# Layer 1: the first of two projections woven into the attention is no longer pinned to score products

## The chip, the cores and the metric

The kernel runs on one core of one Trainium2 chip. The metric is the device time of one execution in microseconds (us). A time given for a kernel is the median of its runs. The profile is of one execution more, and a program's order of instructions on every engine is fixed when it is built: each engine takes its own list from the front.

## The reference

A two-layer backbone over 1024 latent tokens (a grid of 16 rows and 64 columns) and 256 context tokens, model width 1024, all in fp32. Each layer normalizes its input, scales and shifts it, projects it to queries, keys, values and gates, mixes, projects back, and adds to the stream. Layer 0 (even) has two attentions, one global and one in a band. Layer 1 (odd), where the change is, has a convolution branch and a neighbourhood attention, in parallel:

```
def odd_mixer(...):
    cv, cgl, cg, dq, dk, dv, dg = split_cols(h_lat @ w_in, ODD_WIDTHS)
    x_cv, x_cgl, x_cg, x_dq, x_dk, x_dv, x_dg = split_cols(h_ctx @ w_in, ODD_WIDTHS)
    oc = conformer_conv(cv, cgl, cg, dw_w, dw_b, ln_g, ln_b)
    ...
    def d_row(args):      # one grid row of 64 queries, 8 rows of keys around it, 16 columns wide
        bias = rpb[:, dr_idx][:, :, dc_idx] + col_mask[None, None]
        kk = jnp.concatenate([c_dk, kr], axis=1)
        vv = jnp.concatenate([c_dv, vr], axis=1)
        return gqa_attend(qr[:, :, :, None, :], kk, vv, bias)
    ...
    y_lat = jnp.concatenate([oc, od * jax.nn.silu(dg)], axis=-1) @ w_out
```

The attention has 8 heads of width 64. Each query sees the 256 context keys and a window of 8 x 16 grid keys with a bias from a table.

## The kernel before, in words

**Arithmetic.** Every fp32 matrix product is made of three matmuls. An operand is split into a high part (a cast on ScalarE, line 308) and a low part (a subtraction on GpSimd or VectorE, line 311), and `mm3` (lines 328 to 330) issues high x high, high x low and low x high. A weight block is loaded by `load_w` (line 338): a DMA into `wr` (two buffers), a cast to `wh`, a subtraction to `wl` (four buffers each, which hold one block of four pairs of rows).

**The projections of layer 1.** `d_proj(i)` (line 1126) projects heads 2i and 2i+1. With a first weight block it makes Q for the two halves of the latent tokens, then K for both halves and for the context (the matmuls that read `hc`). With a second block it makes, for each half, V and the gate, then V of the context, each followed by small transposes. Each of these ten products takes 24 matmuls: 512 columns wide, 256 for the context. Results leave through the PSUM tag `pp` (two banks), are split on ScalarE and VectorE (`spq`, `spk`, `spv`) and stored to DRAM (`QD`, `KD`, `VD`, `GD`) by the sync queue. `d_proj` is a generator: it yields three times in each product, after two, five and eight of its eight steps of three matmuls, and once more near its end, 31 yields in all. `d_proj(0)` runs beside the convolution and `d_proj(1)` beside the layer norm that follows it. `d_proj(2)` and `d_proj(3)` are woven into the attention.

**The attention of layer 1.** 16 groups (8 heads, two halves of the grid's columns) of seven key tiles each. A group is prepared by `attn_prep` (line 399): three tables `bm` are loaded (two buffers, line 1271), and in `maxes` (line 1296) products `mx` of keys and queries (lines 1304 and 1312) are reduced to row maxima on VectorE (lines 1306 and 1313, the latter with a table `bm` as input). `attn_fin` (line 426) transposes the maxima (`trn`, line 433) and writes them into the query tile `QL` (line 434). Only then can a key tile's score product be finished: it consists of two matmuls into a PSUM bank `st` (two banks), one with `QH` (line 505) and one with `QL` (line 509). A bias is added on VectorE (line 514), ScalarE takes the exponential (line 515, or 517 for the context tiles), the result is split into `ph` and `pl`, and up to three tiles later `flush` issues the three matmuls `ov` with V (lines 456 to 458).

**What sets the order.** The code traces all instructions in one sequence, each with a priority (its place in that sequence). A scheduler then draws up each engine's list, by dependences, buffers and a timeline of its own: of what it holds to be ready, the lowest priority number goes first. Three things steer it. `later(FL[1])`, with FL[1] = -98, gives the woven projection the priority that it would have 98 instructions earlier. `weave` (line 538) advances the attention `nmain` times and spreads `nfill` steps of the projection over these advances. The attention's first 14 advances are the preparation of two groups; from then on every second advance traces one key tile's score product. And a lag pins the projection's matmuls:

```
def weave(main, nmain, fill, nfill, last=True, all_fill=True, lag=0):
    ...
        while done * nmain < (k + 1) * nfill:
            with ExitStack() as cx:
                cx.enter_context(later(FL[layer[0]]))
                if lag and len(sts) >= lag:
                    cx.enter_context(tc.issue_after(sts[-lag].ins))
                next(fill, None)
            done += 1
```

`sts` is the list of all score products traced so far (their first matmuls, line 505), layer 0's too. `issue_after` puts what the step issues on that product's engine, TensorE, behind that product in TensorE's list. It is an order, not a wait for a result, and it does not touch the step's casts, subtractions and DMAs. With a lag of 6, a step cannot be issued ahead of the sixth last score product traced. The calls are

```
weave(main, WV[0], d_proj(2), 31, False, True, LAG[0])     # WV[0] = 77
weave(main, WV[1], d_proj(3), 31, False, True, LAG[1])     # WV[1] = 45
```

and after these the output projection is woven in with LAG[2] and LAG[3].

Of the kernel before, what the change touches and what calls it, by code (L numbers as in the profile page):

```python
# [51 lines left out]
OHQ = 0  # L52
PCB = 3
FL = (80, -98)
LAG = (6, 6, 6, 12)
FIN = (2, 2)
WV = (77, 45, 85, 24, 12)
SQ = (0, 1)
# [30 lines left out]
def tile_kernel(ctx: ExitStack, tc: tile.TileContext, a, out):  # L89
# [448 lines left out]
    def weave(main, nmain, fill, nfill, last=True, all_fill=True, lag=0):  # L538

        done = 0  # L540
        for k in range(nmain):
            next(main, None)
# [7 lines that stand above are left out]
        if all_fill:  # L550
            for _ in fill:
                pass
        if last:
            for _ in main:
                pass
# [458 lines left out]
    with ExitStack() as l1x:  # L1014
# [331 lines left out]
        def out1_alloc():  # L1346
            for c in range(2):
                ocs.append(bigp.tile([P, 2, 4, 512], F32R, tag="big", name=nm("oc")))
            for c in range(2):
                x2.append(bigp.tile([P, DK, 512], F32, tag="big", name=nm("x2")))  # L1350
                od3.append(pair("od3"))
            for c in range(2):
                for f in range(4):
                    lo = ocs[c][:, 1, f, :]
                    SC.dma_start(lo.bitcast(F32), Oc[:, f, c * 512 : (c + 1) * 512])

        def out1_split():
            for _ in range(2):
                yield
            for f in range(4):  # L1360
                for c in range(2):
                    lo = ocs[c][:, 1, f, :]
                    with behind():
                        split(lo.bitcast(F32), ocs[c][:, 0, f, :], lo, "s", "gv"[c])
                if f % 2:
                    yield
# [8 lines left out]
        def od_load(hf):  # L1375
            od[hf] = bigp.tile([P, 2, 3, 512], F32R, tag="big", name=nm("od"))
            for f in range(3):
                split(yo[:, f, hf], od[hf][:, 0, f, :], od[hf][:, 1, f, :], "s", ODE)
# [24 lines left out]
        def out1_part(fs, ks=(0, 1)):  # L1403
            for e2 in range(4):
                w = load_w(wp, a["od_wo"], e2, 256, WB, dks=fs)
                for e in (2 * e2, 2 * e2 + 1):
                    if fs[0] == 0:
                        x2_load(e)
                    for k in ks:
                        yield from out1(fs, e, k, *w)  # L1410
# [59 lines left out]
        main = attn_gen(dlow, groups1, VSH, LOOK1, {11: [], 12: [13, 14], 13: [15]})  # L1470
        weave(main, WV[0], d_proj(2), 31, False, True, LAG[0])
        weave(main, WV[1], d_proj(3), 31, False, True, LAG[1])
        out1_alloc()
        weave(main, WV[2], chain(out1_split(), out1_part(range(4))), 36, False, True, LAG[2])
        assert fin[0] >= 12
        for hf in (1, 0):
            od_load(hf)
        weave(main, WV[3], out1_part((4, 5, 6), (1,)), 8, False, True, LAG[3])
        assert fin[0] >= 14
# [127 lines left out]
```

## Time and profile before

| | |
|---|---|
| three runs | 1565.89, 1562.34, 1564.85 us |
| median | 1564.85 us |
| profiled execution, its time | 1560.63 us |
| its span, first to last instruction | 1558.8 us |
| granted TensorE clock, mean | 0.967 of full speed |

TensorE's busy time counts a matmul from its start to a modelled end, and matmuls overlap: two of 512 columns start about 0.23 us apart and each is shown as 0.39 us long. So a stretch in which TensorE is shown busy throughout can still go at half speed; the granted clock beside it tells that. A row of the order of time gives the start, the length, the engine, the line, and in brackets the idle time before it with what ended it. A name such as `hc`, `hh` or `hl` is an input of the projections (context, high and low part of the latent tokens); `p` is a projection's PSUM tile.

### The profile page before, as it was taken

What the parts mean: (1) busy time and instruction counts of PE and PEld (TensorE: products, weight loads), DVE (VectorE), ACT (ScalarE), POOL (GpSimd) and SP (SyncE); (2) the same over time, 40 slices, a digit from 0 to 9 for tenths busy, and PEclk for the clock granted to TensorE, in tenths of its full rate; (3) what the DMA queues carried; (4) which work ended last, traced back from release to release, by engine and by line L of the source; (5) the groups of instructions that cost most, each with busy time, mean ns of one, the idle gap of its engine ahead of it and who ended that gap; (6) DMA issues with size and microseconds to landing.
All of it is one profiled execution on the core that took longest, in us unless ns stands there. A gap on an engine that the chain in (4) does not pass through costs nothing.

```text
span 1558.8 us, 21469 instructions
## 1 busy us (share of the span) xinstructions
PE 1458.2 (94%) x7084; PEld 1172.0 (75%) x7084; DVE 1053.0 (68%) x2113; ACT 746.6 (48%) x1418; POOL 799.6 (51%) x637
## 2 busy tenths in 40 slices
PE   6899999998998989999999878999999799989995
PEld 2786977896896768876866656888887688868875
DVE  2833557589579865466677946999756566577866
ACT  3721434444435565447556663443434355555563
POOL 3430434455445765557556664665632334364675
PEclk9899999999999999999999989999999899989996
DMA  9474315422312245122112012111446777878632
GB/s 363 160 240 132 106 58 182 143 70 91 118 51 78 94 159 169 54 68 54 47 31 92 7 50 81 51 52 41 149 159 204 208 220 227 256 218 241 182 111 108
DMA packets 154169, 199.83 MB, mean 128 GB/s; under 512 B 14717, under 2 KB 95817, under 8 KB 154057
## 3 DMA queue, kind: packets, MB, share of 16 engines
q1 hardware_dynamic: 147392, 186.88, 38.3%
q10 hardware_dynamic: 6664, 11.57, 2.2%
q8 instruction: 56, 0.92, 0.3%
q14 instruction: 57, 0.46, 0.1%
HBM read 148.07 MB, written 49.02 MB: 126 GB/s over the span
## 4 chain that ended last, share of the span: by engine, by line
PE 74%; DVE 14%; issue 4%; DMA 3%; POOL 2%; ACT 2%; SPq 0%; DVEq 0%; POOLq 0%; ACTq 0%
PE p L328 7%; PE p L329 7%; PE p L330 7%; PE ov L456 4%; PE ov L458 4%; PE ov L457 4%; PE po L329 4%; PE po L328 4%; PE po L330 4%; PE st L505 4%; PE st L509 4%; PE pq L328 2%; PE pq L329 2%; PE pq L330 2%; PE pg L328 2%
## 5 line engine op out<-in xcount | busy, mean ns | idle before, releaser
L311 POOL TENSOR_TENSOR pl<-pf,ph 128x512 fp32r<-128x512 f32 (+4 forms) x321 | 395.2, 1242 | 375.6 <-ACT ph L308 326.3
L517 ACT ACTIVATE pf<-st 128x512 f32<-128x512 f32 x284 | 166.3, 597 | 211.3 <-PE st L509 169.4
L311 POOL TENSOR_TENSOR wl<-wr,wh 128x512 fp32r<-128x512 f32 (+2 forms) x131 | 170.6, 1314 | 144.7 <-ACT wh L308 125.8
L308 ACT CAST ph<-pf 128x512 fp32r<-128x512 f32 (+4 forms) x364 | 209.1, 588 | 27.1 <-PE ov L457 16.9
L328 PE MATMUL p<-hh,wh 128*128 128x512 f32 x448 | 177.6, 397 | 5.6 <-ACT hh L308 2.8
L329 PE MATMUL p<-hl,wh 128*128 128x512 f32 x448 | 176.0, 394 | 1.2 <-POOL hl L311 1.2
L330 PE MATMUL p<-hh,wl 128*128 128x512 f32 x448 | 173.4, 393 | 0.0
L505 PE MATMUL st<-QH,KAt 128*128 128x512 f32 (+4 forms) x364 | 141.5, 390 | 8.9 <-ACT pf L517 8.1
L456 PE MATMUL ov<-ph,Vt 128*128 128x512 f32 (+4 forms) x364 | 141.1, 388 | 5.2 <-DVE y L666 3.9
L458 PE MATMUL ov<-pl,Vt 128*128 128x512 f32 (+4 forms) x364 | 141.1, 388 | 1.8 <-POOL pl L311 1.4
L457 PE MATMUL ov<-ph,Vt 128*64 128x512 f32 (+4 forms) x364 | 139.0, 382 | 0.0
L509 PE MATMUL st<-QL,KBt 68*128 68x512 f32 (+4 forms) x364 | 136.5, 386 | 1.9 <-DVE QL L434 1.8
L1079 DVE SCALAR_TENSOR_TENSOR cps<-U,taps,cps 128x512 f32<-128x512 f32 x184 | 126.4, 751 | 0.9
L308 ACT CAST wh<-wr 128x512 fp32r<-128x512 f32 (+2 forms) x134 | 81.1, 613 | 94.5 <-DMA wr<-in_od_d_dram 18.0
L328 PEld LDWEIGHTS p<-hh,wh 128*128 128x128 f32 x448 | 84.8, 189 | 24.2 <-ACT hh L308 3.0
L329 PEld LDWEIGHTS p<-hl,wh 128*128 128x128 f32 x448 | 84.9, 190 | 19.3 <-POOL hl L311 2.2
L330 PEld LDWEIGHTS p<-hh,wl 128*128 128x128 f32 x448 | 85.0, 190 | 17.3
L629 DVE TENSOR_REDUCE mp<-mx 128x1 f32<-128x512 f32 x128 | 85.3, 681 | 16.6 <-PE mx L628 15.7
L328 PE MATMUL pq<-wh,hh 128*128 128x384 f32 x256 | 88.5, 346 | 2.8 <-ACT hh L308 2.8
L505 PEld LDWEIGHTS st<-QH,KAt 128*128 128x128 f32 x364 | 69.7, 192 | 26.5 <-ACT pf L517 11.6
L948 DVE SCALAR_TENSOR_TENSOR x<-po,modT,x 128x512 f32<-128x512 f32 (+1 forms) x72 | 47.0, 657 | 62.2 <-PE po L330 61.3
L329 PE MATMUL pq<-wl,hh 128*128 128x384 f32 x256 | 87.6, 342 | 0.0
(280 smaller groups left out, 3473.1 us busy)
## 6 DMA issues: line engine op xcount, KB each, us to landing
mw<-in_mod_w_dram SPq DMA_DIRECT2D x16, 1024.0 KB, 5.6
Q<-qs SPq DMA_DIRECT2D x40, 256.0 KB, 2.2
QH<-Q SPq DMA_DIRECT2D x80, 128.0 KB, 2.8
mw<-in_mod_w_dram SPq DMA_DIRECT2D x16, 512.0 KB, 6.8
wr<-in_od_d_dram SPq DMA_DIRECT2D x32, 256.0 KB, 3.6
wr<-in_ev_qkv_dram SPq DMA_DIRECT2D x16, 384.0 KB, 5.3
KAt<-KD SPq DMA_DIRECT2D x16, 384.0 KB, 5.6
wr<-in_od_wo_dram SPq DMA_DIRECT2D x22, 256.0 KB, 3.4
```

What stands on the lines that cost most here:

```text
L308: acts.append(SC.copy(hi, src))
L311: (GP if leng == "g" else VE).tensor_tensor(lo, src, hi.bitcast(F32), op=ALU.subtract)
L328: PE.matmul(o, lh, rh, start=first, stop=False)
L329: PE.matmul(o, lh, rl, start=False, stop=False)
L330: PE.matmul(o, ll, rh, start=False, stop=last)
L456: PE.matmul(o, V[:, 64:192], ph[:, :n], start=(t == 0), stop=False)
L457: PE.matmul(g.ov[0:64, q0 : q0 + n], V[:, 0:64], ph[:, :n], start=False, stop=False)
L458: PE.matmul(o, V[:, 64:192], pl[:, :n], start=False, stop=(last and g.sink is None))
L505: sts.append(PE.matmul(st[:, :n], KA[:, cs], g.QH[:, q0 : q0 + n], start=True, stop=False))
L509: PE.matmul(st[:, :n], KB[0:68, cs], g.QL[0:68, q0 : q0 + n], start=False, stop=True)
L517: acts.append(SC.activation(pf[:, :n], st[:, :n], AF.Exp, scale=1.0 if g.bias else SCALE))
L1079: VE.scalar_tensor_tensor(pc, uc, w, pc, op0=ALU.mult, op1=ALU.add)
```

## The change

One constant: the lag of the first weave, that of `d_proj(2)`, goes from 6 to 0. With 0, `weave` skips the `issue_after`. The priority of 98 instructions earlier stays, as do the lags of the other weaves and all instructions.

```
-LAG = (6, 6, 6, 12)
+LAG = (0, 6, 6, 12)
```

## The prediction

> **What bounds the kernel now.** I read the page first, then busy time by stretches around the place of the change, then TensorE's instructions in order of time, then the waits and the chain there.
>
> ```profile
> span 1558.8 us, 21469 instructions
> ...
> PE 1458.2 (94%) x7084; PEld 1172.0 (75%) x7084; DVE 1053.0 (68%) x2113; ACT 746.6 (48%) x1418; POOL 799.6 (51%) x637
> ...
> PE 74%; DVE 14%; issue 4%; DMA 3%; POOL 2%; ACT 2%; SPq 0%; DVEq 0%; POOLq 0%; ACTq 0%
> ```
>
> TensorE is the bound: 74% of the chain that ended last. An order of work can win only where TensorE stands still or runs at a lower clock. The stretches in which the first woven projection runs (columns: stretch, length, busy of PE, PEld, DVE, ACT, POOL, then granted clock, DMA share, GB/s):
>
> ```profile
> 1212.00:1216.00 4.00, 2.88 (x12) 1.80 (x10) 2.79 (x8) 0.85 (x2) 0.00 (x0) 1.00 1.09 270
> 1216.00:1220.00 4.00, 0.47 (x1) 0.19 (x1) 0.49 (x1) 0.00 (x0) 0.00 (x0) 0.66 1.09 374
> 1220.00:1224.00 4.00, 2.64 (x5) 1.37 (x5) 3.29 (x10) 0.00 (x0) 0.00 (x0) 0.50 0.51 154
> 1224.00:1228.00 4.00, 2.17 (x8) 1.57 (x8) 2.13 (x6) 0.94 (x2) 0.00 (x0) 0.50 0.42 112
> 1228.00:1232.00 4.00, 4.00 (x17) 3.58 (x17) 2.73 (x5) 2.91 (x7) 3.49 (x4) 0.63 0.27 75
> 1230.00:1281.00 51.00, 51.00 (x279) 43.78 (x279) 33.10 (x82) 31.08 (x63) 24.64 (x24) 0.99 0.70 200
> 1281.00:1362.00 81.00, 81.00 (x432) 69.12 (x431) 48.97 (x116) 40.36 (x84) 32.67 (x30) 1.00 0.82 250
> ```
>
> There is a hole from 1213 to 1228, with the clock down to half. After it TensorE is full without a break through both woven projections, up to 1362. TensorE's own order in and behind the hole:
>
> ```profile
> 1210.73 0.28 PE L505 MATMUL st<-QH,KAt 128*128 128x256 f32 x1
> 1210.85 0.40 PE L328 MATMUL p<-hh,wh 128*128 128x512 f32 x1
> 1211.09 0.40 PE L329 MATMUL p<-hl,wh 128*128 128x512 f32 x1
> ...
> 1213.15 0.39 PE L1304 MATMUL mx<-KAt,QH 128*128 128x256 f32 x2
> 1213.86 0.96 PE L1312 MATMUL mx<-KAt,QH 128*128 128x320 f32 x2 [0.31 <-DVE mp L1313]
> 1215.26 0.50 PE L1304 MATMUL mx<-KAt,QH 128*128 128x256 f32 x2 [0.44 <-DVE mp L1313]
> 1216.54 0.47 PE L1312 MATMUL mx<-KAt,QH 128*128 128x440 f32 x1 [0.78 <-DVE mp L1306]
> 1220.99 0.73 PE L1312 MATMUL mx<-KAt,QH 128*128 128x440 f32 x1 [3.98 <-DVE mp L1313]
> ...
> 1223.41 0.64 PE L1312 MATMUL mx<-KAt,QH 128*128 128x320 f32 x1 [0.27 <-DVE mp L1306]
> ...
> 1226.22 0.98 PE L509 MATMUL st<-QL,KBt 68*128 68x512 f32 x2 [1.83 <-DVE QL L434]
> ...
> 1228.13 0.49 PE L509 MATMUL st<-QL,KBt 68*128 68x352 f32 x1
> 1228.43 0.41 PE L328 MATMUL p<-hc,wh 128*128 128x256 f32 x1
> ...
> 1230.13 0.63 PE L509 MATMUL st<-QL,KBt 68*128 68x512 f32 x1
> 1230.56 0.55 PE L1312 MATMUL mx<-KAt,QH 128*128 128x440 f32 x1
> ...
> 1232.22 0.31 PE L509 MATMUL st<-QL,KBt 68*128 68x320 f32 x1
> 1232.37 0.28 PE L328 MATMUL p<-hc,wh 128*128 128x256 f32 x1
> 1232.49 0.28 PE L329 MATMUL p<-hc,wh 128*128 128x256 f32 x1
> ```
>
> The attention cannot start. Its row maxima (mx) are reduced on VectorE with tables that a DMA brings (bm, two buffers), and the second halves of the score products (L509) need those maxima in QL. Two products' first halves have taken both st banks, so no third score product can be issued before 1226. What makes the hole, from the waits (total, times, longest) and then from the chain (start, length):
>
> ```profile
> POOL pl L311 <- ACT ph L308: 27.7, 1, 27.7
> ACT pf L517 <- PE st L509: 11.8, 1, 11.8
> ...
> DVE mx L1313 <- DMA bm<-in_d_bm_dram: 4.7, 2, 3.9
> ```
>
> ```profile
> 1215.05 5.19 DMA bm<-in_d_bm_dram
> ...
> 1222.48 2.19 DMA bm<-in_d_bm_dram
> ```
>
> **Does the pin hold work back here?** By the code, the weave spreads 31 steps of the projection over 77 advances of the attention. The first 14 advances are preparation, then every second one traces a key tile. Counting both from 0, step 11 is traced when 7 tiles are, and is pinned behind tile 1; step 12 behind tile 2 (8 traced), step 13 behind tile 4 (10 traced). Steps 0 to 9 are pinned behind products of layer 0, long done. The trace agrees at each place: nine matmuls start right behind tile 1's product (1210.85); the next, the context part of K (hc), stand still over the whole hole and start at 1228.43, right behind tile 2's pair; the next nine at 1232.37, right behind tile 4's. So the pin is what leaves the hole empty. hc's weights were already there, being those of the K matmuls before it.
>
> **The sum, on the profiled execution.** Its own time is 1560.63 us (span 1558.8 and 1.8 around it); the median of the three runs shown, 1564.85, is 4.2 higher. The forecast is the difference put on that median. The measurement can tell about 0.2%, 3.1 us, from no change.
>
> *Removed:* an order on TensorE alone. No instruction goes or comes; loads, casts and stores were never pinned, but they wait for the matmuls that free their buffers and so move with them.
>
> *Room in the hole:* the idle pieces above, 0.31 + 0.44 + 0.78 + 3.98 + 0.27 + 1.83 = 7.6 us. Besides, from 1226.22 to 1230.56 the products start 0.43 us apart (1230.13 to 1230.56) where warm ones start 0.24 apart (1210.85 to 1211.09): 4.3 us of work that takes 2.4 warm, so 1.9 more. Together 9.5.
>
> *What can fill it:* K's context part, 24 matmuls 0.12 apart (1232.37 to 1232.49): 2.9 us. Then the first V block, 24 at 0.24: 5.8. Together 8.7. V needs the second weight block:
>
> ```profile
> L311 POOL TENSOR_TENSOR wl<-wr,wh 128x512 fp32r<-128x512 f32 x6 | 7.7, 1294 | 4.2 <-ACT wh L308 2.9 <-PE p L329 1.3
> ...
> L308 ACT CAST wh<-wr 128x512 fp32r<-128x512 f32 x6 | 3.7, 614 | 4.3 <-DMA wr<-in_od_d_dram 2.8 <-PE p L329 1.4
> ```
>
> ```profile
> wr<-in_od_d_dram SPq DMA_DIRECT2D x8, 256.0 KB, 4.3
> ```
>
> Its buffers come free as hc's matmuls pass, from about 1214.3. Each of four pairs then takes a cast of 0.61 and a subtraction of 1.29. ScalarE and GpSimd idle there for 11.8 and 27.7 us, so this is hidden; had they been full, it would cost 4 x 1.9. Two raw pairs are staged by their two buffers. The other two must be loaded: about 1215 + 4.3 + 1.9 = 1221.2, inside the hole. So 8.7 us of fill fits, by data. The DVE half of hc's split and its store on SP also move in; VectorE waits 3.9 us there itself.
>
> *What comes through:* work done in the hole is gone from the full stretch behind it, but the attention must be able to use that. Score products per stretch (first halves, the x in brackets), and the last idle piece of the one in which the attention ran almost alone:
>
> ```profile
> 1227.50:1281.00 53.50, 8.54 (x23) 4.65 (x24) 0.97 0.68 193
> ...
> 1353.00:1373.00 20.00, 3.71 (x10) 1.88 (x10) 0.91 0.86 263
> 1362.00:1381.00 19.00, 3.48 (x8) 1.78 (x8) 0.82 1.00 278
> ```
>
> ```profile
> 1378.50 0.77 PE L1304 MATMUL mx<-KAt,QH 128*128 128x256 f32 x2 [3.71 <-DMA KAt<-KD]
> ```
>
> Now it goes at 53.5/23 = 2.33 us a tile, TensorE full. With 8.7 us less work TensorE would allow 44.8/23 = 1.95. Almost alone, the attention managed 20/10 = 2.0, and in the other stretch 19/8 = 2.38, or 1.91 without the 3.71 us wait for K, which this stretch does not have. With fill still between, neither end is reached: I take 2.1, nearer to 2.0, because that row has the fewer foreign waits. That gives 23 x (2.33 - 2.1) = 5.2 us. Ends: 23 x (2.33 - 2.0) = 7.5, and nothing at 2.38.
>
> *What it costs:* two weight loads of 256 KB come while the DMA engines are full (1.09 and 374 GB/s at 1216 to 1220), together with the bm tables on which the chain waits: 524 KB / 374 GB/s = 1.4 us on that chain. Between none and this I take all.
>
> *Sum:* -5.2 + 1.4 = -3.8 us: 1556.8 for the profiled execution, **1561.0 us** against the median. Behind 1281 the second projection is still pinned and TensorE full (81.00 of 81), so the shift should reach the end. What is late next is the attention's own chain.
>
> **A rule of the skill that speaks against it.** The row of 3.98 us shows the head of TensorE's order waiting and nothing passing it. The Trainium skill, "TensorE: Matmul & The Clock Gate", Part 3 ("What overlaps and what doesn't"), says that matmuls keep program order strictly, only weight loads may run ahead; this case's trace agrees as far as the 3.98 us row goes. By it, a V matmul put into the hole and waiting for its weights would hold up the maxima behind it; that is rival C (1570.0 against 1561.0).
>
> **The rivals.**
> A, all of it comes through: the attention keeps up at 1.95 us a tile and the loads disturb nothing. For it: VectorE is busy 33.1 and ScalarE 31.1 of 51 us there. Against: no stretch shows a pace under 2.0 without taking a wait out. Gain 8.7 to 9.5: about 1555.7.
> B, it is given back: freed of pins, the fill is used up before tile 26, and the second projection still waits behind tile 26. The attention then runs alone, at 2.38 a tile with a lowered clock (0.82 in that row). At a mean pace of 2.33 nothing is left: 1564.85, or 1566.3 with the loads' 1.4.
> C, slower: V matmuls stand in the order ahead of the maxima, and their last weight pair comes late. The maxima wait for bm until 1220.24 (1215.05 + 5.19); the last pair is ready at about 1221.2 undisturbed, 1223.9 with a further subtraction of 1.3 and the 1.4 of contention. It decides when the pair is later than bm: up to 3.7 us on the attention's start, with nothing gained since TensorE waits too; with the loads' 1.4 added to bm's second round, 5.1: 1570.0.
> That the pin does nothing is excluded by the three places above.
>
> **How the numbers follow.** Forecast (gain 1 to 7.5) 0.48; A 0.11; B 0.21; C 0.20. Of the forecast's own range about three quarters lie beyond 3.1 us: faster 0.36 + 0.11 = 0.47. Same: the other 0.12 and most of B, 0.18: 0.30. Slower: C and a little of B: 0.23. The range runs from 1553.5, the whole room of 9.5 and 1.8 more for half the spread of the runs shown (1562.34 to 1565.89), to 1568.5, short of C's end; the forecast's own is 1557.3 to 1563.9.
>
> **What would show it.** Right: hc matmuls between 1213 and 1220, no idle piece near 4 us before the first L509, the clock near 1 in 1216 to 1228, no full stop of TensorE up to the end of the second projection, which ends 3 to 5 us earlier. Loads: bm's wait on VectorE longer than 4.7 us. B: idle TensorE just before tile 26, and the second projection starting at the same time as now. C: TensorE waiting for wl or wh in the hole, and the first L509 later than 1226.2. The forecast is wrong if the hole stays open, or if it fills and the second projection's end does not move.

## The result and the profile after

| | before | after |
|---|---|---|
| median | 1562.34 us (11 runs) | 1571.16 us (11 runs) |
| lowest to highest | 1558.21 to 1565.89 | 1565.62 to 1573.50 |
| profiled execution, its time | 1560.63 us | 1567.64 us |
| its span | 1558.8 us | 1565.9 us |

The changed kernel is slower: ratio 1.0048, 95% interval 1.0033 to 1.0064. The forecast was 3.8 us faster: 1561.0 us, put on the median of the three runs shown with it (1564.85), with a range from 1553.5 to 1568.5. A ratio here and below is worked out over all executions and is not the quotient of the two medians; three single executions far out (2052.9 us of the kernel before, 3605.55 of e1_lag12, 3608.42 of e12_wv) are left out of the ratios.

The page of the changed kernel: span, busy time, and the shares of the chain of waits that ended last. The totals hardly say more than that the span grew by 7.1 us, so the places have to be read.

```profile
span 1565.9 us, 21471 instructions
...
PE 1463.2 (93%) x7084; PEld 1174.2 (75%) x7084; DVE 1049.3 (67%) x2113; ACT 748.0 (48%) x1418; POOL 803.0 (51%) x637
...
PE 74%; DVE 14%; DMA 4%; issue 3%; POOL 2%; ACT 1%; SPq 0%; DVEq 0%; POOLq 0%; ACTq 0%
```

The changed kernel by stretches (stretch, length, busy time of PE, PEld, DVE, ACT and POOL with instruction counts, granted clock, DMA share, GB/s). The first five answer to the same stretches of before; the others were chosen from the order below.

```profile
1212.00:1216.00 4.00, 4.00 (x29) 3.72 (x29) 1.63 (x4) 1.82 (x4) 0.78 (x1) 1.00 1.11 324
1216.00:1220.00 4.00, 4.00 (x23) 3.49 (x23) 1.83 (x5) 0.55 (x2) 1.77 (x2) 1.00 1.08 371
1220.00:1224.00 4.00, 4.00 (x20) 3.31 (x19) 1.91 (x7) 0.77 (x2) 1.29 (x1) 1.00 0.81 254
1224.00:1228.00 4.00, 4.00 (x21) 3.32 (x20) 1.51 (x5) 0.47 (x1) 1.29 (x1) 1.00 0.63 162
1228.00:1232.00 4.00, 3.19 (x18) 2.35 (x17) 2.69 (x8) 2.79 (x6) 0.00 (x0) 1.00 0.38 104
1231.00:1255.00 24.00, 24.00 (x135) 20.64 (x133) 13.81 (x32) 13.83 (x28) 10.18 (x10) 1.00 0.55 171
1254.80:1289.40 34.60, 26.98 (x97) 18.82 (x95) 23.52 (x60) 16.69 (x35) 14.55 (x15) 0.75 0.77 215
1289.00:1371.00 82.00, 81.74 (x422) 69.14 (x422) 46.54 (x112) 40.23 (x82) 29.68 (x28) 0.98 0.75 222
```

The hole is closed: TensorE is full from 1212 to 1228 and the clock is 1.00, where it was down to 0.50. But a new slack stretch stands at 1254.8 to 1289.4: TensorE busy 27.0 of 34.6 us at a clock of 0.75. TensorE's order of time in the changed kernel shows how the one led to the other:

```profile
1185.66 1.05 PE L265 MATMUL bc<-ident,nr 128*128 128x128 f32 x8
...
1213.66 0.29 PE L328 MATMUL p<-hc,wh 128*128 128x256 f32 x1
...
1225.75 0.40 PE L1304 MATMUL mx<-KAt,QH 128*128 128x256 f32 x2
...
1226.92 0.31 PE L1312 MATMUL mx<-KAt,QH 128*128 128x320 f32 x1
...
1228.91 0.31 PE L1312 MATMUL mx<-KAt,QH 128*128 128x320 f32 x1
...
1230.58 0.62 PE L509 MATMUL st<-QL,KBt 68*128 68x512 f32 x2 [0.81 <-DVE QL L434]
...
1231.63 0.39 PE L328 MATMUL p<-hh,wh 128*128 128x512 f32 x1
...
1236.16 0.33 PE L505 MATMUL st<-QH,KAt 128*128 128x352 f32 x1
...
1254.47 0.28 PE L330 MATMUL p<-hc,wl 128*128 128x256 f32 x1
...
1254.78 0.31 PE L505 MATMUL st<-QH,KAt 128*128 128x320 f32 x1
...
1289.41 0.55 PE L505 MATMUL st<-QH,KAt 128*128 128x224 f32 x1 [0.26 <-DVE pf L514]
...
1289.97 0.66 PE L328 MATMUL p<-hh,wh 128*128 128x512 f32 x1
```

The matching places of the kernel before: the last broadcast of the layer norm ahead of the attention (a common zero ahead of the change), the third tile's score product (tile 2 when counted from 0) and tile 26's, and the second projection's first matmul.

```profile
1185.36 1.05 PE L265 MATMUL bc<-ident,nr 128*128 128x128 f32 x8
...
1227.67 0.66 PE L505 MATMUL st<-QH,KAt 128*128 128x352 f32 x1
...
1281.33 0.27 PE L505 MATMUL st<-QH,KAt 128*128 128x224 f32 x1
...
1281.92 0.47 PE L328 MATMUL p<-hh,wh 128*128 128x512 f32 x1
```

What is to be seen, in order:

1. hc's matmuls now start at 1213.66, in the hole. So far the forecast.
2. They are not alone. In TensorE's list 313 projection matmuls stand ahead of the third tile's product, against 221 before (both counted from one fixed place, 125 matmuls ahead of the first woven projection's own): 92 more, where the forecast had 48. They are K's context part, the first V, the first gate, and most of the second V.
3. The first pair with QL comes at 1230.58 instead of 1226.22, and behind it 20 more projection matmuls (from 1231.63) stand ahead of the third tile, at 1236.16 instead of 1227.67: 8.5 us later, or 8.2 counted from the broadcast.
4. The fill is used up at tile 11 (1254.78). The second projection is still pinned, and starts right behind tile 26 (1289.97 behind 1289.41). Between the two the attention is alone: 15 tiles in 34.6 us, 2.31 each.
5. Tile 26 is 8.1 us late (1289.41 against 1281.33), and from there both kernels have the same work on a full TensorE: 81.74 of 82.0 busy, as 81.00 of 81 before. Little of the delay is absorbed behind it: the span ends 7.1 us later.

Who waits for whom in the hole: the kernel before, from 1215 to 1227,

```profile
DVE mx L1313 <- DMA bm<-in_d_bm_dram: 4.7, 2, 3.9
DVE mp L1306 <- PE mx L1304: 0.2, 1, 0.2
```

and the changed kernel, from 1215 to 1231 (idle time of VectorE: total, times, longest).

```profile
DVE mx L1313 <- PE mx L1312: 3.9, 3, 2.1
...
DVE mp L1306 <- PE mx L1304: 1.9, 1, 1.9
DVE mx L1313 <- DMA bm<-in_d_bm_dram: 0.5, 1, 0.5
```

Before, VectorE waited 4.7 us for the tables bm and 0.2 for TensorE's products of the maxima. Now it waits 0.5 for the tables and 5.8 for the products, which stand in TensorE's list behind projection matmuls (1225.75, 1226.92 and 1228.91 above). The Trainium skill, "TensorE: Matmul & The Clock Gate", Part 3 ("What overlaps and what doesn't"), has matmuls in strict program order; these rows agree: a maxima product of 0.3 us is late by what stands ahead of it.

And TensorE's waits while the attention is alone (1254.5 to 1289.5), in the changed kernel:

```profile
PE mx L1304 <- DMA QH<-QD: 2.1, 1, 2.1
PE mx L1312 <- DVE mp L1313: 1.6, 2, 1.2
PE ov L456 <- DVE yo L1329: 1.4, 2, 0.8
PE ov L458 <- POOL pl L311: 1.1, 1, 1.1
```

No one of them is large enough to be the cause by itself; most are steps of the attention's own chain from engine to engine, with no fill left to cover them. But that chain alone does not account for the whole stretch. The same 15 tiles, 11 to 26, take 34.0 us in the kernel before, with 90 projection matmuls between them, and 29.1 us in the run with no fill at all (e7_alone, below), at a clock of 0.80. The changed kernel needs 34.6 without any. What slows it by the other 5.5 us is not shown.

### The profile page after: what moved, and what is told of

Same layout as the page of the kernel before. It is cut to its first block, busy times and chain, and to the rows that moved or that the text cites. A ratio compares the mean times of both kernels' runs of the same rounds, so it can differ in the third digit from the quotient of the medians.

```text
span 1565.9 us, 21471 instructions
## 1 busy us (share of the span) xinstructions
PE 1463.2 (93%) x7084; PEld 1174.2 (75%) x7084; DVE 1049.3 (67%) x2113; ACT 748.0 (48%) x1418; POOL 803.0 (51%) x637
## 4 chain that ended last, share of the span: by engine, by line
PE 74%; DVE 14%; DMA 4%; issue 3%; POOL 2%; ACT 1%; SPq 0%; DVEq 0%; POOLq 0%; ACTq 0%
PE p L328 7%; PE p L330 7%; PE p L329 7%; PE ov L456 4%; PE ov L458 4%; PE ov L457 4%; PE po L328 4%; PE po L329 4%; PE po L330 4%; PE st L505 4%; PE st L509 4%; PE pq L328 3%; PE pq L330 3%; PE pq L329 3%; PE pg L328 2%
## 5 line engine op out<-in xcount | busy, mean ns | idle before, releaser
L517 ACT ACTIVATE pf<-st 128x512 f32<-128x512 f32 x284 | 166.3, 597 | 205.2 <-PE st L509 159.8
L328 PE MATMUL p<-hh,wh 128*128 128x512 f32 x448 | 178.1, 398 | 5.6 <-ACT hh L308 2.8
L509 PE MATMUL st<-QL,KBt 68*128 68x512 f32 (+4 forms) x364 | 136.5, 386 | 0.9 <-DVE QL L434 0.8
L329 PEld LDWEIGHTS p<-hl,wh 128*128 128x128 f32 x448 | 85.2, 190 | 19.6 <-POOL hl L311 2.2
L458 PEld LDWEIGHTS ov<-pl,Vt 128*128 128x128 f32 x364 | 71.0, 195 | 25.1 <-POOL pl L311 6.8
L456 PEld LDWEIGHTS ov<-ph,Vt 128*128 128x128 f32 x364 | 71.2, 196 | 23.5 <-issue 5.1
```

Source lines behind the costliest of these rows:

```text
L328: PE.matmul(o, lh, rh, start=first, stop=False)
L329: PE.matmul(o, lh, rl, start=False, stop=False)
L456: PE.matmul(o, V[:, 64:192], ph[:, :n], start=(t == 0), stop=False)
L458: PE.matmul(o, V[:, 64:192], pl[:, :n], start=False, stop=(last and g.sink is None))
L509: PE.matmul(st[:, :n], KB[0:68, cs], g.QL[0:68, q0 : q0 + n], start=False, stop=True)
L517: acts.append(SC.activation(pf[:, :n], st[:, :n], AF.Exp, scale=1.0 if g.bias else SCALE))
```

## The experiments

Three theories to begin with. **G**, given back: the fill is used up early, the second projection is still pinned behind tile 26, and the attention alone leaves TensorE slack. **S**: the late start alone is the loss. **P**: the attention's own pace, about 2.3 us a tile, is the bound, so that work done in the hole is worth nothing in any order. Each ratio is to the kernel before, of runs on the same chip. The list at the end puts all runs side by side.

### The lag doubled instead of removed (e1_lag12)

```
-LAG = (6, 6, 6, 12)
+LAG = (12, 6, 6, 12)
```

> The first weave's lag is 12 tiles instead of 6 or none; nothing else differs. In TensorE's order 39 more projection matmuls than before stand ahead of the third tile's product (260 against 221; in the changed kernel 313), and the projection is used up by tile 22 (changed kernel: tile 11). Theory G (give-back: the loss is the attention running alone while the second projection is still pinned behind tile 26): the alone stretch shrinks from 15 tiles to 4 or 5, so nearly all of what the hole takes (about 6.5 us of matmuls) stays: 2 to 5 us faster than before. Theory S (late start: matmuls standing ahead of the maxima push the attention's start, and everything hangs on that start): 39 matmuls, 6.5 us, in a room of 9.5 us delay the start by 1 to 2 us: 1 to 2 us slower than before, with tile 26 as late as the first tiles.

Measured 1564.53 us, ratio 1.0006 (0.9988 to 1.0023): no difference that can be told. 260 matmuls ahead of the third tile, which is no later than before. G's gain did not appear; P would fit.

### The second projection unpinned as well (e2_both)

```
-LAG = (6, 6, 6, 12)
+LAG = (0, 0, 6, 12)
```

> The changed kernel with the second projection's pin taken away too (lags 0, 0, 6, 12). The start of the attention is the same as in the changed kernel (313 projection matmuls ahead of the third tile); the second projection now begins at tile 14 instead of behind tile 26. Theory G: the idle time of TensorE between tiles 11 and 26 (36 us at a clock of 0.75) is filled; tile 50 comes 7 to 12 us earlier than in the changed kernel, and the time falls by as much, to 1 to 5 us below before. Theory S: the start is as late as in the changed kernel, so the end is too: 6 to 8 us slower than before.

Measured 1558.01 us, ratio 0.9982 (0.9964 to 1.0000), about 10 us below the changed kernel's ratio. TensorE in this kernel, from the third tile to tile 26:

```profile
1235.10:1294.50 59.40, 59.12 (x315) 49.88 (x314) 38.83 (x94) 32.88 (x67) 24.70 (x23) 1.00 0.72 211
```

The start is as late as in the changed kernel (313 matmuls ahead of the third tile, 50.5 us from the broadcast in both), yet the loss is gone. TensorE is full at a clock of 1.00 and 470 projection matmuls are done by tile 26 instead of 365. So S falls as the only cause.

### The second weave begun earlier, the second lag kept (e3_early)

```
-LAG = (6, 6, 6, 12)
-WV = (77, 45, 85, 24, 12)
+LAG = (0, 6, 6, 12)
+WV = (50, 72, 85, 24, 12)
```

> The changed kernel with the two weaves' shares of the attention moved: 50 and 72 advances instead of 77 and 45, same sum. The second projection is still pinned (lag 6) but its first step is traced 13 tiles earlier and spread over more tiles: it begins at tile 13 and is drawn out to tile 50. The attention's start is as late as in the changed kernel. Theory G: as in the run without both pins, 7 to 12 us faster than the changed kernel, 1 to 5 us faster than before, since TensorE has fill through the whole stretch. Theory S: no gain, 6 to 8 us slower than before.

Measured 1560.07 us, ratio 0.9986 (0.9970 to 1.0002). The same cure by another way: 461 matmuls by tile 26. G again, against S.

### The priority of the first weave far behind the attention (e4_gap)

```
-    def weave(main, nmain, fill, nfill, last=True, all_fill=True, lag=0):
+    def weave(main, nmain, fill, nfill, last=True, all_fill=True, lag=0, prio=None):
...
-                    cx.enter_context(later(FL[layer[0]]))
+                    cx.enter_context(later(prio if prio is not None else FL[layer[0]]))
...
-        weave(main, WV[0], d_proj(2), 31, False, True, LAG[0])
+        weave(main, WV[0], d_proj(2), 31, False, True, LAG[0], 2000)      # LAG[0] = 0
```

> The changed kernel with the first projection's priority put 2000 places later instead of 98 earlier, so that the scheduler uses it only where nothing of the attention is ready on its timeline. Its order has 293 projection matmuls ahead of the third tile instead of 313, and is used up at tile 12 as in the changed kernel. If the priority is what pushes the attention's start, the third tile's product comes 4 to 8 us earlier than in the changed kernel and the time falls by as much, to before or below. If it is the scheduler's timeline (it takes the maxima for not ready longer than they are), the order hardly changes: the start is at most 4 us earlier, and the time stays 3 us or more above before. Theory G has the alone stretch unchanged (tiles 12 to 26, 33 to 36 us) in either case.

Measured 1575.56 us, ratio 1.0083 (1.0059 to 1.0108), slower than the changed kernel. Still 293 matmuls stand ahead of the third tile, which comes 50.4 us from the broadcast (50.5 in the changed kernel). So it isn't the priority of 98 instructions earlier that lets the fill overtake. The scheduler takes the lowest number among what it holds to be ready; that its timeline holds the maxima to be later than they are on the chip is what remains, but that is argued, not shown.

### Both lags doubled (e5_12_12)

```
-LAG = (6, 6, 6, 12)
+LAG = (12, 12, 6, 12)
```

> Lag 12 in both weaves (12, 12, 6, 12). The first 23 tiles have the order of the run with lag 12 in the first weave alone (39 projection matmuls more in the hole, the third tile on time at 1227.7); the second projection then goes on at tile 23 instead of behind tile 26. Theory G (what the hole takes is given back while the second projection is pinned): nothing is given back now, the 6.5 us stay: 4 to 7 us faster than before, tile 50 about 5 us earlier than before. Theory P (the attention cannot go faster than about 2.3 us a tile anyway, so work done in the hole is worth nothing, and the gain of the run without both pins came from elsewhere): tile 50 where it was, time within 2 us of before.

Measured 1561.40 us, ratio 1.0007 (0.9992 to 1.0023). G's gain is missed a second time.

### The attention with no fill at all (e7_alone)

Both projections are made ahead of the attention, which is thereby measured alone.

```
-        weave(main, WV[0], d_proj(2), 31, False, True, LAG[0])
-        weave(main, WV[1], d_proj(3), 31, False, True, LAG[1])
+        run(d_proj(2))
+        run(d_proj(3))
+        weave(main, WV[0] + WV[1], iter(()), 0, False)
```

> Both projections are traced ahead of the attention instead of woven in: all 384 remaining projection matmuls stand ahead of the third tile, and tiles 2 to 57 run with no fill at all. It measures the attention's own pace, which the prediction took as 2.1 us a tile (ends 2.0 and 2.38). If the prediction's term was mis-sized, the pace is 2.2 to 2.35, as in the alone stretches of the changed kernel (2.31) and of the run without both pins (2.20), with a granted clock under 0.9; if the prediction's term was right, 1.9 to 2.1. The time is much longer than before in either case, by 40 to 65 us, since TensorE then stands idle for half of the attention.

Measured 1605.52 us, ratio 1.0288 (1.0270 to 1.0307). The third tile to tile 26 in this kernel:

```profile
1314.40:1358.60 44.20, 36.41 (x138) 25.69 (x138) 28.93 (x72) 26.57 (x52) 22.12 (x22) 0.77 0.70 193
```

24 tiles in 44.2 us: 1.84 a tile, well under P's 2.3. P falls: with TensorE free of fill the attention does go faster, and what is taken off the full stretch is worth something, down to 44 us.

### The lag doubled and the second weave begun earlier; each alone; and further (e9_12_wv, e12_wv, e11_12_wv60)

```
-LAG = (6, 6, 6, 12)
-WV = (77, 45, 85, 24, 12)
+LAG = (12, 6, 6, 12)
+WV = (67, 55, 85, 24, 12)
```

> Lag 12 in the first weave, 6 in the second, and the weaves' shares 67 and 55 instead of 77 and 45, so that the second projection, still pinned, can begin at about tile 21 instead of 27. 54 more projection matmuls than before stand in front of the third tile, about 9 us, as much as the room in the hole. Theory G: little is given back: 3 to 7 us faster than before. Theory P: within 2 us of before. If the start is late (third tile after 1229), it is 1 to 3 us late, and by G costs nothing, since TensorE has fill until tile 50.

Measured 1556.63 us, ratio 0.9975 (0.9962 to 0.9988): faster than both kernels. The control has the lag of before and the same second weave:

```
-WV = (77, 45, 85, 24, 12)
+WV = (67, 55, 85, 24, 12)
```

> Control: the kernel before with lag 6 in both weaves and only the shares moved to 67 and 55. The hole stays nearly empty (227 matmuls ahead of the third tile against 221), but the second projection starts about 6 tiles earlier (401 by tile 26 against 365). If the gain of the run with lag 12 and these shares came from the hole's fill being kept, this one gains nothing: within 2 us of before. If it came from the earlier second projection alone, this one is 3 to 5 us faster too.

Measured 1564.86 us, ratio 1.0015 (1.0000 to 1.0031). So the earlier second weave gives nothing by itself (227 matmuls ahead of the third tile, the hole open), nor does the doubled lag by itself (1.0006): they gain together. One step further, with more ahead of the third tile (293 instead of 275):

```
-LAG = (6, 6, 6, 12)
-WV = (77, 45, 85, 24, 12)
+LAG = (12, 6, 6, 12)
+WV = (60, 62, 85, 24, 12)
```

> As the run with lag 12 and shares 67 and 55, but 60 and 62: the second projection begins at tile 18; 72 more matmuls than before ahead of the third tile (293 against 221), 63 more by tile 26 (428 against 365). Theory G: the start is 3 to 5 us late, which costs nothing as long as TensorE has fill: 3 to 6 us faster than before, like the run with 67 and 55. If a late start costs by itself (theory S), 1 to 4 us slower than that run.

Measured 1564.64 us, ratio 1.0014 (0.9998 to 1.0031): the gain is gone. By the ratios it is about 6 us slower than the run with 67 and 55. G missed, and it is more than S had; the start was 0.8 us later than in that run (46.9 us from the broadcast against 46.1), so a late start does not explain it.

### The forecast's own fill, and no more (e10_room)

Only steps 12 to 17 of the first weave are freed, which are K's context part and the first V: the 48 matmuls of the forecast. All later steps keep the lag of 6.

```
-    def weave(main, nmain, fill, nfill, last=True, all_fill=True, lag=0):
+    def weave(main, nmain, fill, nfill, last=True, all_fill=True, lag=0, free=0):
...
-                    if lag and len(sts) >= lag:
+                    if lag and done >= free and len(sts) >= lag:
...
-        weave(main, WV[0], d_proj(2), 31, False, True, LAG[0])
+        weave(main, WV[0], d_proj(2), 31, False, True, LAG[0], 18)      # LAG[0] = 6
```

> The kernel before, with the pin taken from steps 12 to 17 of the first projection alone: K's context part and the first V block, 48 matmuls, just the fill that the prediction summed for the hole (269 ahead of the third tile against 221); the other steps keep lag 6, the second projection is as before. The prediction's sum, if right: start of the attention at most 1.4 us late, tile 26 5 us earlier, 3 to 5 us faster. Theory G: the start is on time or up to 1.5 us late, but tile 26 comes no earlier than before (53 us behind the third tile, as in all of before, the changed kernel and the run with lag 12), because the attention does not use TensorE's free time, and the second projection waits behind tile 26: within 2 us of before.

Measured 1558.55 us against 1562.12, ratio 0.9975 (0.9958 to 0.9992): 3.9 us faster, where the forecast had 3.8. The order ahead of the third tile has 269 matmuls, 48 more than before. The hole and the stretch from the third tile to tile 26 in this kernel:

```profile
1213.00:1230.00 17.00, 14.46 (x68) 10.90 (x67) 8.19 (x23) 3.94 (x9) 5.10 (x4) 0.90 0.81 253
...
1231.00:1280.50 49.50, 48.10 (x249) 38.47 (x250) 35.23 (x88) 29.80 (x60) 21.51 (x21) 1.00 0.69 202
```

and its order of time at the same places as above:

```profile
1186.25 1.05 PE L265 MATMUL bc<-ident,nr 128*128 128x128 f32 x8
...
1229.78 0.61 PE L509 MATMUL st<-QL,KBt 68*128 68x512 f32 x2
...
1230.91 0.43 PE L505 MATMUL st<-QH,KAt 128*128 128x352 f32 x1 [0.17 <-DVE pf L514]
...
1280.53 0.28 PE L505 MATMUL st<-QH,KAt 128*128 128x224 f32 x1
```

Counted from the broadcast, the third tile is 2.4 us later than before (44.66 against 42.31). From there to tile 26 it takes 49.6 us instead of 53.7 (1281.33 - 1227.67): 2.07 us a tile. The forecast had taken 1.4 and 2.1. So tile 26 comes 1.7 us earlier (94.28 against 95.97 from the broadcast), which G, as it was put ahead of this run, had excluded. The whole gain lies up to tile 11, where 6 projection matmuls are left of 54: 14.6 us instead of 19.6. From tile 11 to tile 26 both have 90 matmuls, and this kernel takes 35.0 us against 34.0.

The fill did not all find its data in the hole. The third pair's low part ends at 1224.62 and releases a projection matmul (the wait of 0.62 us), and the fourth pair's ends at 1227.27. TensorE's row, and then GpSimd's:

```profile
1224.68 0.80 PE L330 MATMUL p<-hh,wl 128*128 128x512 f32 x1 [0.62 <-POOL wl L311]
```

```profile
1223.35 1.27 POOL L311 TENSOR_TENSOR wl<-wr,wh 128x512 fp32r<-128x512 f32 x1 [4.96 <-ACT wh L308]
1226.00 1.27 POOL L311 TENSOR_TENSOR wl<-wr,wh 128x512 fp32r<-128x512 f32 x1 [1.38 <-ACT wh L308]
```

Counted from the broadcast, the forecast had both pairs ready at 35.8 us (1221.2 - 1185.36); they came at 38.4 and 41.0.

### The changed kernel's start without its lonely stretch (e13_free24)

Steps 0 to 23 are free, so that the same 313 matmuls stand ahead of the third tile as in the changed kernel; the last 52 keep the lag and are spread up to tile 26.

```
-        weave(main, WV[0], d_proj(2), 31, False, True, LAG[0])
+        weave(main, WV[0], d_proj(2), 31, False, True, LAG[0], 24)      # weave as above, LAG[0] = 6
```

> Only the steps 0 to 23 of the first weave are free of the pin, steps 24 to 30 keep the lag of 6. By TensorE's order 313 projection matmuls then stand ahead of the third tile's product, as in the changed kernel, so the attention starts as late as there (first product with QL 4 to 5 us, third tile about 8 us later than before, counted from the last layer norm broadcast). But the last 52 matmuls are spread up to tile 26 instead of being used up at tile 11. Theory G (the loss is the stretch from tile 11 to tile 26 in which the attention is alone, at a clock of 0.75): that stretch is gone, tile 2 to tile 26 take 44 to 47 us instead of 53.3, and the time is 0 to 3 us below the kernel before (1559 to 1562.5). Theory S (the late start alone makes the loss): tile 2 to tile 26 take 52 to 54 us again and the time is 6 to 9 us above the kernel before, as that of the changed kernel.

Measured 1564.43 us against 1561.35, ratio 1.0020 (1.0008 to 1.0032): between the two theories, below the changed kernel and above the kernel before. Stretch and order of this kernel:

```profile
1241.00:1288.60 47.60, 40.28 (x203) 32.57 (x202) 33.37 (x84) 27.77 (x54) 19.92 (x19) 0.89 0.65 185
```

```profile
1187.70 1.05 PE L265 MATMUL bc<-ident,nr 128*128 128x128 f32 x8
...
1241.15 0.33 PE L505 MATMUL st<-QH,KAt 128*128 128x352 f32 x1
...
1288.65 0.27 PE L505 MATMUL st<-QH,KAt 128*128 128x224 f32 x1
```

The third tile to tile 26 takes 47.5 us (1288.65 - 1241.15) instead of the 53.25 of the changed kernel (1289.41 - 1236.16): G's part is real. Of these 5.75 us, 3.8 lie up to tile 11, where 4 matmuls stand instead of 52, and 1.9 behind it, though 48 matmuls stand there and none in the changed kernel. But the start is 53.5 us from the broadcast instead of 42.3, and 47.5 us does not pay for it: there are too few matmuls left to move, for the attention alone takes 44.2. The start is 3 us later here than in the changed kernel (50.5), though TensorE's order ahead of it is the same. The trace shows a stop in the hole that the changed kernel does not have:

```profile
1223.10 0.51 PE L328 MATMUL p<-hh,wh 128*128 128x512 f32 x1 [2.66 <-DVE spk L311]
```

A projection matmul waits 2.66 us for VectorE to read the context part of K out of its PSUM bank; VectorE waits there for ScalarE, which waits 5.6 us for the store `KD<-spk`. Behind the stop the granted clock is 0.8. This profiled execution took 1567.56 us, 3.1 above its kernel's median, so the stop need not be in the others. Without the 3 us, tile 26 would by estimate still be 2.0 us later than before (50.5 + 47.5 against 42.3 + 53.7).

### The forecast's fill with the second weave begun earlier (e14a)

```
-WV = (77, 45, 85, 24, 12)
+WV = (67, 55, 85, 24, 12)
...
-        weave(main, WV[0], d_proj(2), 31, False, True, LAG[0])
+        weave(main, WV[0], d_proj(2), 31, False, True, LAG[0], 18)      # weave as above, LAG[0] = 6
```

> Steps 12 to 17 free of the pin (48 matmuls, the forecast's own fill) and the second weave begun ten advances earlier (67 and 55 instead of 77 and 45): 269 projection matmuls ahead of the third tile, 404 ahead of tile 26. Each part alone: steps 12 to 17 free 0.9975, the earlier weave alone 1.0015. If what is done in the hole is kept by any later order that leaves no stretch without fill (theory G): 3 to 7 us below the kernel before. If the earlier weave costs what it cost alone, because it slows the tiles before 26: 0 to 3 us below.

Measured 1567.97 us against 1561.35, ratio 1.0042 (1.0026 to 1.0058): slower, a miss of both expectations. The stretch from the third tile to tile 26, in this kernel and then in the faster one with the lag of 12 and the same second weave:

```profile
1235.50:1299.70 64.20, 60.67 (x290) 48.81 (x291) 39.11 (x97) 33.92 (x66) 25.88 (x24) 0.95 0.64 187
```

```profile
1234.30:1293.20 58.90, 57.25 (x290) 47.72 (x291) 39.72 (x93) 32.19 (x66) 25.58 (x24) 0.97 0.68 209
```

The same count of TensorE instructions (290) takes 5.3 us longer in one order than in the other, at nearly the same clock. No single wait carries it. Why is open; so the counts below explain the large differences, not every one of 0.2 to 0.4%.

### All runs side by side

Matmuls: projection matmuls in TensorE's list ahead of the third tile and ahead of tile 26. Times in us, of one profiled execution each: third tile counted from the last broadcast ahead of the attention (L265), then third tile to tile 26, and tile 50 counted from that broadcast. The profiled executions took from 7.0 us less (e1_lag12) to 5.0 us more (e3_early) than the medians of their kernels, so a few us in these three columns need not be those of the ratio.

| run | matmuls ahead of third tile, tile 26 | third tile | to tile 26 | tile 50 | ratio |
|---|---|---|---|---|---|
| before | 221, 365 | 42.3 | 53.7 | 174.7 | 1 |
| after | 313, 365 | 50.5 | 53.3 | 183.0 | 1.0048 |
| e1_lag12 | 260, 365 | 42.6 | 53.1 | 174.2 | 1.0006 |
| e2_both | 313, 470 | 50.5 | 59.5 | 166.3 | 0.9982 |
| e3_early | 313, 461 | 52.3 | 59.1 | 173.9 | 0.9986 |
| e4_gap | 293, 365 | 50.4 | 56.7 | 186.3 | 1.0083 |
| e5_12_12 | 260, 392 | 42.3 | 57.8 | 171.9 | 1.0007 |
| e7_alone | 605, 605 | 122.5 | 44.2 | 218.7 | 1.0288 |
| e9_12_wv | 275, 413 | 46.1 | 59.0 | 172.4 | 0.9975 |
| e10_room | 269, 365 | 44.7 | 49.6 | 172.3 | 0.9975 |
| e11_12_wv60 | 293, 428 | 46.9 | 65.0 | 174.2 | 1.0014 |
| e12_wv | 227, 401 | 42.6 | 64.1 | 178.1 | 1.0015 |
| e13_free24 | 313, 365 | 53.5 | 47.5 | 179.1 | 1.0020 |
| e14a | 269, 404 | 45.0 | 64.3 | 179.4 | 1.0042 |

All reach 605 by tile 50. The runs with 365 at tile 26 are the ones to compare: they differ only in how 144 matmuls are laid out before and between. Where the counts at tile 26 differ, tile 50 is the place to compare. It comes 2.3 and 2.4 us earlier than before in e9_12_wv and e10_room, the two fastest, and 3 to 12 us later in every run that is 0.15% or more slower (e7_alone aside). It is not the whole account: in e2_both it is 8.4 us earlier for a gain of 0.18%, and in e5_12_12 2.8 us earlier for none.

## Why the prediction was wrong

**The step that failed:** "So 8.7 us of fill fits, by data." The prediction chose K's context part and the first V as what would go into the hole, and then took this choice for what would go in. Nothing limits the fill to these two: the first gate and the second V need the same second weight block as the first V. With the pin gone, 92 matmuls went in instead of 48, in about 9.5 us of room, and the 52 left were used up by tile 11.

**That this is the step** is shown by the run that frees the forecast's 48 and no more: it gave -0.25% (-3.9 us; interval -0.08 to -0.42%) where the changed kernel gave +0.48%. That the forecast had -3.8 for it is in part luck, for its terms do not add up to it on the trace:
- *the pin holds hc back:* right, hc's matmuls start at 1213.66 in the changed kernel.
- *room 7.6 + 1.9 us, and the data in time:* too large. The 48 matmuls (8.7 us of work) moved the third tile by 2.4 us, so the hole took in 6.3 of them. The two weight pairs that have to be loaded were ready 2.5 and 5.2 us later than the 1221.2 that the forecast had for both.
- *pace 2.1 us a tile:* 2.07 with 96 matmuls between the third tile and tile 26. But the forecast set 2.1 against 2.33 over 23 tiles, a gain of 5.2 us; measured over 24 tiles it is 2.07 against 2.24, a gain of 4.1.
- *cost 1.4 us of the loads:* the start moved by 2.4. No run shows the term as it was meant, for VectorE's wait for bm fell, from 4.7 us to 1.9 in that run (1215 to 1231) and to 0.5 in the changed kernel. Instead maxima products stood behind fill in TensorE's list: VectorE waited 1.9 us for them in that run and 5.8 in the changed kernel.

So at tile 26 the gain is 4.1 - 2.4 = 1.7 us, not 3.8. At tile 50 it is 2.4 and at the end of the span 3.1 (both counted from the broadcast); the rest is within the interval, about 1 to 7 us.

**The loss in two parts,** by the ratios: from the forecast's fill (0.9975) to the same order ahead of the third tile as in the changed kernel, with the rest still pinned (1.0020), is +0.45%, about 7.0 us, for 44 matmuls more ahead of the third tile; from there to the changed kernel (1.0048) is +0.28%, about 4.4 us, for using up the last 52 by tile 11. With the gain of 3.9: -3.9 + 7.0 + 4.4 = 7.5 us, which is 0.48% of 1562. Each part is uncertain by about 0.2%, 3 us, so which of the two is larger is not shown.

**Why the 44 aren't paid back:** fill between the third tile and tile 26 is nearly free while it is little. 0 matmuls there take 44.2 us (the attention alone), 52 take 47.5, 96 take 49.6, 144 take 53.7 (before); e1_lag12, with 105, took 53.1. From 96 down to 52 only 2.1 us are won, where the start was put back by 8.8 us (53.5 against 44.7; 5.8 without the stop told above). The prediction bounded the pace by 1.95 to 2.38 us a tile, but didn't ask how much fill the attention can lose before its own chain is the bound.

**The rivals.** B named the mechanism of the second part: fill used up before tile 26, the second projection pinned, TensorE idle at a lowered clock. But it was priced at 1566.3 at most, because it let the start stand where it was. C named the late start, up to 5.1 us, but by late weights; TensorE did not wait for weights in the changed kernel's hole (in e10_room it did, for 0.6 us). The start came 8.5 us late from projection matmuls that stood in the list ahead of the maxima. The case that came about is B and the late start together, which were kept as two alternatives. Of the signs that the prediction named, the closed hole and the clock came out as for a gain, and the stop ahead of tile 26, the second projection starting no earlier, and the first L509 later than 1226.2 as for B and C.

**What stays open:** why the scheduler places the fill ahead of the maxima (the priority was excluded; its timeline is argued, not shown), why the changed kernel's 15 tiles without fill take 34.6 us where e7_alone takes 29.1, and what the order does in e9_12_wv, e11_12_wv60 and e14a, which lie up to 0.7% apart. e1_lag12 and e5_12_12 fill the hole in part (260) and gain nothing; that fits neither G nor the counts alone.

## What to carry to other kernels

A pin or a lag that leaves a hole may also be what rations the fill. Before removing it, list everything that becomes ready, not only what would fit, and ask what the stretch behind will run on when that is gone. Here it was best to free about as much as the hole holds and keep the rest pinned: six steps freed gave -0.25%, all of them +0.48%. It is no rule by itself: the same six steps with the second weave begun earlier gave +0.42%.

Work moved ahead of a chain's start must come back as a shorter stretch behind it; its limit is the chain alone (44.2 us here), which one run without any fill measures. Where the rest of the fill is to be had (the second projection unpinned too), the same late start cost nothing.

## What was not expected of the hardware

The granted clock fell to half with no long idle piece. The changed kernel's lonely stretch in slices of 3 us (columns as in the stretches above), and the longest idle piece in it:

```profile
1269.00:1272.00 3.00, 1.95 (x6) 1.72 (x7) 2.00 (x5) 1.55 (x4) 1.01 (x2) 0.50 1.11 278
1272.00:1275.00 3.00, 2.60 (x9) 1.86 (x7) 2.62 (x8) 0.00 (x0) 0.61 (x1) 0.50 0.68 224
1275.00:1278.00 3.00, 2.22 (x6) 1.22 (x6) 2.96 (x12) 2.60 (x4) 1.03 (x1) 0.50 0.73 198
1278.00:1281.00 3.00, 3.00 (x10) 2.53 (x11) 1.65 (x3) 1.54 (x5) 1.11 (x2) 0.50 0.88 244
```

```profile
1270.05 0.79 PE L1304 MATMUL mx<-KAt,QH 128*128 128x256 f32 x2 [2.13 <-DMA QH<-QD]
```

The clock is 0.50 for 12 us (1269 to 1281), in which TensorE is shown busy for 9.8 (1.95 + 2.60 + 2.22 + 3.00), and no idle piece is longer than 2.13 us. The Trainium skill, "TensorE: Matmul & The Clock Gate", Part 1 ("HAM oscillation — how this bites in real kernels"), gives as its abstract rule no idle gap over about 3.4 us. Here that was not enough: a stretch with few matmuls (27 in these 12 us; the four slices count those across a border twice) stayed at half clock with gaps below it.
